# Two transformer blocks on one core: fp32 attention products as split fp32r products, and low parts of weights by adding transfers

## The chip, the cores and the metric

The kernel runs on one core of a Trainium2 chip. Its engines are TensorE (PE: matrix products and transposes, with the load of its stationary operand shown apart as PEld), VectorE (DVE), ScalarE (ACT), GpSimd (POOL) and SyncE (SP). Each executes its own instructions in a fixed order and waits on semaphores for the others. The metric is the device time of one execution in microseconds; before the change it is 1470.13 us, the median of three runs from 1469.56 to 1470.28.

## The reference

512 tokens of width 1024 pass two transformer blocks in fp32. Block 1 has two mixers, gated linear attention and a sparse attention (NSA: attention to compressed keys, to all earlier keys and to a window, with a softmax in each), and a gated feed-forward of width 2816. Block 2 has two short causal convolutions and a stick-breaking attention side by side, and a feed-forward of width 4096.

```python
# block 1
proj = rms_norm(x) @ w_in              # all projections of both mixers
x = x + rms_norm(mixed @ w_out)        # mixed: both mixers' outputs, gated
x = x + rms_norm((silu(h @ w_gate) * (h @ w_up)) @ w_down)
# block 2
p = _rmsnorm(x, g_attn) @ w_in         # a_b, a_c, a_h, b_glu, q, k, v
y_a = a_b * _causal_dwconv(a_c * a_h, w_conv_a)                    # 3 taps
y_b = silu(_layernorm(_causal_dwconv(glu(b_glu), w_conv_b) + b))   # 31 taps
x = x + concat([y_a, y_b, y_c]) @ w_out
x = x + square(relu(_rmsnorm(x, g_ffn) @ w_ff1)) @ w_ff2
```

y_c is the stick-breaking attention, eight heads of 64:

```python
def _stick_breaking(q, k, v):
    t_len = q.shape[2]
    scale = 1.0 / math.sqrt(q.shape[-1])
    outs = []
    for q0 in range(0, t_len, SB_BLOCK):
        kv_len = q0 + SB_BLOCK
        qb = q[:, :, q0:kv_len]
        kb = k[:, :, :kv_len]
        vb = v[:, :, :kv_len]
        z = jnp.einsum("bhqd,bhkd->bhqk", qb, kb).astype(jnp.float32) * scale
        t_idx = q0 + jnp.arange(SB_BLOCK)[:, None]
        s_idx = jnp.arange(kv_len)[None, :]
        mask = s_idx < t_idx
        log_beta = jax.nn.log_sigmoid(z)
        log_1m = jnp.where(mask, log_beta - z, 0.0)
        suffix = lax.cumsum(log_1m, axis=3, reverse=True) - log_1m
        a = jnp.where(mask, jnp.exp(log_beta + suffix), 0.0)
        outs.append(jnp.einsum("bhqk,bhkd->bhqd", a.astype(v.dtype), vb))
    return jnp.concatenate(outs, axis=2)
```

## The kernel before

A weight arrives in fp32 as a tile of 512 KB on SP's queue (`load`, L121, four buffers `wst`). `split_w` (L108) makes two tiles of type fp32r of it: the high part `whi` by a cast on ACT (L113) and the low part `wlo`, weight minus high part, on DVE (L114), four buffers each. Activations are split the same way (`split_psum`, L134 to L141, from PSUM: cast at L137, subtract at L138). A product of two fp32 matrices is then three fp32r products into one PSUM bank: high by high, low activation by high weight, high activation by low weight. `k_steps` (L160 to L162) does this for an output of 128 features by 512 tokens, eight weight blocks deep; `nat_steps` (L197 to L199) for one of 128 tokens by 512 features. Both are generators that give control back after each three products.

Some products of the attentions are not split but have fp32 operands. In block 1, `nsa_values` multiplies the values by the transposed weights of four key blocks; for the last block (b = 3, 128 columns) it uses an fp32 copy `VF` of the values and an fp32 `PTf` (L825), 16 times in all, while the other blocks use split parts. In block 2, `sb_scores` computes for every head and every query block j the scores z of 128 queries by 128 (j + 1) keys from fp32 `QF` and `KF` (L1076), and adds the causal mask by a bf16 product with an identity (L1077). ACT and DVE then turn z into weights: three functions on ACT (L1081 to L1083), a subtraction and a scan on DVE (L1085, L1086), an exp on ACT (L1089). `sb_values` transposes the weights on PE (L1114), splits them and multiplies them with the values, for the last key block from fp32 `VB3` (L1103). A trace shows an fp32 product as two records. In NSA's scores (L792) the width is a maximum of n and 256, so that none has fewer columns than that.

The order of the work in block 2's mixers is written as generators. `first_tiles` runs the first four weight tiles while the last norm of block 1 still transposes into hT (L384). Then a loop over the eight heads takes turns: a step of the head's values, some steps of `fill`, a convolution tap on DVE, a step of the next head's scores. `fill` is the sequence of everything else that PE has to do there: `v_steps` (v's columns in four chunks of 512 KB, used four times over), then pairs 1 to 3 of q and k, the convolutions' inputs (`glu_steps`, `gate_steps`), and the first part of the output projection. From the program in this order the framework's scheduler derives each engine's list, in which instructions may move against the written order; the lists are fixed before the run.

The norms go through ACT (squares, L349), POOL (`rstd`, L356 and L357) and DVE (`xn`, L378), then through PE's transposes.

Of the kernel before, what the change touches and what calls it, by code (L numbers as in the profile page):

```python
# [7 lines left out]
F32 = mybir.dt.float32  # L8
# [12 lines left out]
def kernel(  # L21
# [404 lines left out]
    VF = to("VF", shape=(128, 4, 64))  # L426
# [21 lines left out]
    def products(t):  # L448
        acc = ps("mm" if t < 3 else "s")
        nat_mm(hT_k, acc[:, 0:NM], t, wm)  # L450
        src = acc[:, 0:256].rearrange("p (b g d) -> p b g d", b=2, g=2)
        V.tensor_copy(misc[:, t, :], acc[:, 256:NM])
        split_psum(VS[:, t, :, :, 0, :], VS[:, t, :, :, 1, :], src)
        if t == 3:
            A.copy(VF.rearrange("p a d -> p (a d)"), acc[:, 0:256])

# [354 lines left out]
    def nsa_values(h, bi):  # L811

        g = h // 4
        tt = weights.pop((h, bi))
        parts = []

        def products():
            b, rhs = parts.pop(0)
            if b == 3:
# [12 lines left out]
        for b in (3, 2, 1, 0):  # L832
            n = 512 - 128 * b
            pt = ps("pt", "pt")
            for j in range(b, 4):
                nc.tensor.transpose(pt[:, (j - b) * 128:(j - b + 1) * 128],
                                    tt[j][:, b * 128:(b + 1) * 128], ident)
            if b < 3:
                ph = tS("PTh", F32R, bufs=2)
                pl = tS("PTl", F32R, bufs=2)  # L840
                split_psum(ph[:, 0:n], pl[:, 0:n], pt[:, 0:n])
                parts.append((b, (ph, pl)))
            else:
                pf = tS("PTf", shape=(128, 128), bufs=2)
                A.copy(pf, pt[:, 0:n])
                parts.append((b, (pf,)))
# [98 lines left out]
    def fin_mix(t, half, acc):  # L945
# [16 lines left out]
    identb = tc3("identb", BF16, (128, 128))  # L962
    V.tensor_copy(identb, ident)
    smask = tc3("smask", BF16, (128, 128))
    P.memset(smask, 0.0)
    P.affine_select(out=smask, in_=smask, compare_op=OP.is_gt, fill=-SBIG, base=0,
                    pattern=[[-1, 128]], channel_multiplier=1)
    cwa = tc3("cwa", shape=(128, 2, 3))
    cwb = tc3("cwb", shape=(128, 2, 31))

    def conv_weights():
        for src, dst, k in ((w_conv_a_2, cwa, 3), (w_conv_b_2, cwb, 31)):
            cn = t2("cn", shape=(k, 256))
# [70 lines left out]
    def pair_qk(i, accs):  # L1044
        QF[i], KF[i] = t3("QF", bufs=2), t3("KF", bufs=2)
        A.activation(QF[i], accs[0], AF.Copy, scale=0.125)
        A.copy(KF[i], accs[1])

    def pair_steps(i):
        accs = []  # L1050
        yield from tile_steps(accs, 1280 + i * 128)
        QF[i] = t3("QF", bufs=2)
        A.activation(QF[i], accs[0], AF.Copy, scale=0.125)
        yield from tile_steps(accs, 1792 + i * 128)
        KF[i] = t3("KF", bufs=2)
        A.copy(KF[i], accs[1])

    def v_steps():
        chunks = [([k, k + 1], load(w_in_2, k, 2, 2304, 512)) for k in range(0, 8, 2)]
        for t in range(4):  # L1060
            acc = ps()
            yield from nat_steps(hT_k, acc, t, chunks)
            src = acc.rearrange("p (h d) -> p h d", h=8)
            split_psum(VB[t][:, :, 0, :], VB[t][:, :, 1, :], src)
            if t == 3:
                A.copy(VB3, src)

    def sb_scores(h):

        i, u = h // 2, h % 2  # L1070
        r = slice(u * 64, u * 64 + 64)
# [21 lines left out]
    def sb_values(h):  # L1093
# [7 lines left out]
        def products(b, ph, pl):  # L1101
            if b == 3:
                mm(o[0:64, 384:512], VB3[:, h, :], ph, start=False, stop=False)  # L1103
                return
# [5 lines left out]
        for b in range(4):  # L1110
# [4 lines left out]
            if b < 3:  # L1115
                ph = t3("PTh", F32R, bufs=2)
                pl = t3("PTl0", F32R) if b == 0 else t3("PTl", F32R, bufs=2)
                split_psum(ph[:, 0:n], pl[:, 0:n], pt[:, 0:n])
                parts.append((b, ph, pl))
                pl0 = pl if b == 0 else pl0  # L1120
            else:
                pf = t3("PTf", shape=(128, 128))
                A.copy(pf, pt[:, 0:n])
                parts.append((b, pf, None))
# [8 lines left out]
        pv_evac(o, sby[0][r], t3("pvt", shape=(64, 512)))  # L1133
# [22 lines left out]
    def sigmoid(src):  # L1156
        th = t3("gth")
# [51 lines left out]
    def gate_steps(a):  # L1209
# [5 lines left out]
        m = t3("gam", shape=(128, 544))  # L1215
# [24 lines left out]
    pair_qk(0, accs[:2])  # L1240
    table("natural_log_exp_and_others")
    glu(0, accs[2:])

# [4 lines left out]
    fill = sequence(v_steps(), pair_steps(1), glu_steps(1), pair_steps(2), pair_steps(3), gate_steps(0),  # L1248
# [7 lines left out]
    for h in range(8):  # L1256
        scores = sb_scores(h + 1) if h < 7 else iter(())
        values = sb_values(h)
        for j in range(4):
            steps(values)  # L1260
            steps(fill, 2)
# [7 lines left out]
            steps(fill, 2)  # L1269
# [9 lines left out]
    def fp32_tile(t, h):  # L1279
        tag, bufs = (("QF", 2), ("KF", 2), ("sbe", 3), ("sbL", 2))[2 * h + t // 2]  # L1280
# [107 lines left out]
```

## Time and profile before

| | us |
|---|---|
| median of three runs | 1470.13 (1469.56 to 1470.28) |
| the profiled execution's own time | 1469.14 |
| its span, first to last instruction | 1467.4 |
| PE busy | 1448.1 (99%) |
| PEld busy | 1233.0 (84%) |
| DVE busy | 977.2 (67%) |
| ACT busy | 731.4 (50%) |
| POOL busy | 64.5 (4%) |
| mean granted clock of TensorE | 0.998 |

The span is the time from the first to the last instruction; busy time counts the time in which an engine executes at least one. PE's durations overlap, since products are pipelined: what one takes from PE is read from its start to the start of the next. Block 1's NSA attention lies between 255 and 410 us; block 2's first tiles end at about 912, its v products at 939, the heads at 1080.

### The profile page before, as it was taken

How to read it: one execution, taken by the hardware profiler on the slowest of the kernel's cores; microseconds unless marked ns; L12 is line 12 of the kernel's file. 1: busy time of each engine (PE TensorE's matmuls, PEld its weight loads, DVE VectorE, ACT ScalarE, POOL GpSimd, SP SyncE). 2: the span in 40 equal slices, each digit the busy share in tenths (PEclk: the TensorE clock that was granted, in tenths of full speed). 3: DMA queues.
4: the chain of work that ended last, by engine and by line, in shares of the span. 5: the costliest groups of instructions: out<-in, count | busy, mean ns of one | idle time of the engine just before them, and what ended most of it. 6: DMA issues, size and time to landing. Idle time of an engine off the chain costs nothing. (4 is left out here: it accounts for less than half of the span.)

```text
span 1467.4 us, 21573 instructions
## 1 busy us (share of the span) xinstructions
PE 1448.1 (99%) x8484; PEld 1233.0 (84%) x8484; DVE 977.2 (67%) x1607; ACT 731.4 (50%) x1294; POOL 64.5 (4%) x176
## 2 busy tenths in 40 slices
PE   8999999999999999999999999999999999999998
PEld 6788888787788889899889978766679989898996
DVE  5446556877755479579569845979767748384663
ACT  6434334666633266455335535577746527163453
POOL 2000002000000020000000021000101000000001
PEclk9999999999999999999999999999999999999999
DMA  8242222211133322324233522221122324233331
GB/s 235 74 115 58 73 73 72 58 44 58 44 115 115 113 74 88 119 83 115 87 114 97 179 71 79 80 59 58 58 86 58 115 75 131 83 92 109 88 130 58
DMA packets 181294, 133.30 MB, mean 91 GB/s; under 512 B 11765, under 2 KB 157239, under 8 KB 181192
## 3 DMA queue, kind: packets, MB, share of 16 engines
q1 hardware_dynamic: 181192, 131.92, 30.5%
q8 instruction: 67, 1.10, 0.3%
q14 instruction: 35, 0.29, 0.1%
HBM read 129.80 MB, written 2.10 MB: 90 GB/s over the span
## 5 line engine op out<-in xcount | busy, mean ns | idle before, releaser
L113 ACT CAST whi<-wst 128x1024 fp32r<-128x1024 f32 (+1 forms) x229 | 238.8, 1046 | 293.7 <-PE nat L187 140.1
L114 DVE TENSOR_TENSOR wlo<-wst,whi 128x1024 fp32r<-128x1024 f32 (+1 forms) x229 | 278.6, 1220 | 107.0 <-ACT whi L113 105.7
L263 PE MATMUL ps<-T,whi 128*128 128x256 f32 x1088 | 198.1, 283 | 0.9 <-ACT prod L299 0.9
L185 PE MATMUL nat<-whi,ah 128*128 128x512 f32 (+1 forms) x440 | 171.7, 390 | 0.0
L186 PE MATMUL nat<-wlo,ah 128*128 128x512 f32 (+1 forms) x440 | 171.2, 389 | 0.0
L187 PE MATMUL nat<-whi,al 128*128 128x512 f32 (+1 forms) x440 | 170.5, 390 | 0.0
L263 PEld LDWEIGHTS ps<-T,whi 128*128 128x128 f32 x1088 | 167.0, 188 | 1.4 <-ACT prod L299 1.3
L263 PE MATMUL ps<-T,wlo 128*128 128x256 f32 x544 | 153.2, 282 | 0.9 <-DVE wlo L114 0.9
L149 PE MATMUL ps<-hTh,whi 128*128 128x512 f32 (+1 forms) x336 | 115.9, 345 | 0.0
L150 PE MATMUL ps<-hTl,whi 128*128 128x512 f32 (+1 forms) x336 | 114.9, 342 | 0.0
L151 PE MATMUL ps<-hTh,wlo 128*128 128x512 f32 (+1 forms) x336 | 114.5, 341 | 0.0
L263 PEld LDWEIGHTS ps<-T,wlo 128*128 128x128 f32 x544 | 102.6, 189 | 1.0 <-DVE wlo L114 1.0
L187 PEld LDWEIGHTS nat<-whi,al 128*128 128x128 f32 x440 | 82.8, 188 | 18.7 <-DVE al L339 0.8
L185 PEld LDWEIGHTS nat<-whi,ah 128*128 128x128 f32 x440 | 82.8, 188 | 18.7 <-ACT ah L338 1.0
L160 PE MATMUL ps<-hTh,whi 128*128 128x512 f32 x240 | 98.0, 408 | 0.0
L186 PEld LDWEIGHTS nat<-wlo,ah 128*128 128x128 f32 x440 | 82.8, 188 | 17.7
L161 PE MATMUL ps<-hTl,whi 128*128 128x512 f32 x240 | 96.1, 400 | 0.0
L162 PE MATMUL ps<-hTh,wlo 128*128 128x512 f32 x240 | 95.8, 399 | 0.0
L1226 DVE TENSOR_TENSOR xt<-xt,nat 128x512 f32<-128x512 f32 x43 | 29.5, 685 | 79.0 <-PE nat L187 77.7
L263 PE MATMUL ps<-hTh,whi 128*128 128x256 f32 x272 | 76.9, 283 | 0.3 <-ACT whi L113 0.3
L263 PE MATMUL ps<-hTh,wlo 128*128 128x256 f32 x272 | 76.5, 281 | 0.0
L263 PE MATMUL ps<-hTl,whi 128*128 128x256 f32 x272 | 76.5, 281 | 0.0
(410 smaller groups left out, 3240.0 us busy)
## 6 DMA issues: line engine op xcount, KB each, us to landing
wst<-in_w_in_dram SPq DMA_DIRECT2D x70, 512.0 KB, 3.7
wst<-in_w_ff_dram SPq DMA_DIRECT2D x64, 512.0 KB, 4.3
wst<-in_w_ffn_gate_dram SPq DMA_DIRECT2D x22, 512.0 KB, 4.1
wst<-in_w_ffn_up_dram SPq DMA_DIRECT2D x22, 512.0 KB, 4.9
wst<-in_w_ffn_down_dram SPq DMA_DIRECT2D x22, 512.0 KB, 4.3
wst<-in_w_out_dram SPq DMA_DIRECT2D x16, 512.0 KB, 3.6
xt<-in_x_dram SPq DMA_DIRECT2D x8, 512.0 KB, 3.6
wst<-in_w_proj_gla_dram SPq DMA_DIRECT2D x8, 512.0 KB, 4.2
```

Source lines behind the costliest of these rows:

```text
L113: A.copy(hi, st)
L114: lo_eng[0].tensor_tensor(out=lo, in0=st, in1=hi.bitcast(F32), op=OP.subtract)
L149: mm(acc[:, ts], wh[:, k, cols], xh[:, k, ts], start=k == 0, stop=False)
L150: mm(acc[:, ts], wh[:, k, cols], xl[:, k, ts], start=False, stop=False)
L151: mm(acc[:, ts], wl[:, k, cols], xh[:, k, ts], start=False, stop=k == nk - 1)
L160: mm(acc, w[0][:, k], hT[0][:, k], start=k == 0, stop=False)
L161: mm(acc, w[0][:, k], hT[1][:, k], start=False, stop=False)
L162: mm(acc, w[1][:, k], hT[0][:, k], start=False, stop=k == 7)
L185: mm(acc, ah[:, s], wh[:, j, cols], start=i == 0, stop=False)
L186: mm(acc, ah[:, s], wl[:, j, cols], start=False, stop=False)
L187: mm(acc, al[:, s], wh[:, j, cols], start=False, stop=i == len(seq) - 1)
L263: mm(acc, w[a][:, k0 + k], x[b][:, k], start=first and k + i == 0, stop=last and k == 3 and i == 2, skip_group_check=True)
```

## The change

The fp32 products go. QF and KF become split parts: K is split for both heads of a pair at once (`Kh`, `Kl`), and Q into four zero-padded tiles of 128 rows, high and low for either head (`QZ`, named Qh and Ql in the lists). z is three fp32r products over 128 rows, and mask and identity are fp32r. The last key block's products use split values and split weights as the other blocks do, in both attentions. In a pair, k's tile now comes ahead of q's.

A part of the weights gets its low part in another way: ACT makes the high part (L135 of the changed kernel) and its negative (L136, into `wlo`), and a transfer on POOL's queue (L140) adds the weight from HBM to it. This holds for every second of the 22 tiles that follow the first four in block 2's mixers: two of v's four chunks, then one in two up to the output projection's first half. `wst` is still loaded, for the cast. In `fill`, gate 0 comes ahead of pair 3, and the steps per turn differ for some heads.

```diff
+    adding = [iter(())]
...
+        if next(adding[0], False):
+
+            hi, lo = (base.tile([128, kt, n], F32R, name=nm, tag=nm, bufs=4) for nm in ("whi", "wlo"))
+            A.copy(hi, st)
+            A.activation(lo, hi.bitcast(F32), AF.Copy, scale=-1.0)
+            for i in range(kt if step > 1 else 1):
+                k, j = (k0 + i * step, slice(i, i + 1)) if step > 1 else (k0, slice(0, kt))
+                src = w[k * 128:(k + j.stop - j.start) * 128, c0:c0 + n].rearrange("(k p) c -> p k c", p=128)
+                P.dma_start(out=lo[:, j], in_=src, accum_op=OP.add)
+            return hi, lo
...
-    VF = to("VF", shape=(128, 4, 64))
...
-                if bi == 0:
-                    o[0] = ps("o", "o")
-                    lhs = VCB[g][:, h % 4].rearrange("p a d -> p (a d)")
-                    mm(o[0], lhs, PCT[g][0], start=True, stop=False)
-                    mm(o[0], lhs, PCT[g][1], start=False, stop=False)
-                mm(o[0][0:64, b * 128:512], VF[:, 2 * bi + g, :], rhs[0], start=False, stop=False)
-                return
...
+            ph = tS("PTh", F32R, bufs=2)
+            pl = tS("PTl", F32R, bufs=2)
+            split_psum(ph[:, 0:n], pl[:, 0:n], pt[:, 0:n])
+            parts.append((b, (ph, pl)))
...
-    identb = tc3("identb", BF16, (128, 128))
-    V.tensor_copy(identb, ident)
-    smask = tc3("smask", BF16, (128, 128))
-    P.memset(smask, 0.0)
-    P.affine_select(out=smask, in_=smask, compare_op=OP.is_gt, fill=-SBIG, base=0,
+    identr = tc3("identr", F32R, (128, 128))
+    V.tensor_copy(identr, ident)
+    smask = tc3("smask", F32R, (128, 128))
+    mask = t2("cn", shape=(128, 256))[:, 0:128]
+    P.memset(mask, 0.0)
+    P.affine_select(out=mask, in_=mask, compare_op=OP.is_gt, fill=-SBIG, base=0,
                     pattern=[[-1, 128]], channel_multiplier=1)
+    V.tensor_copy(smask, mask)
...
-    QF, KF = {}, {}
+    KF = {}
-    VB3 = t3("VB3", shape=(128, 8, 64))
...
+    QZ = [[t3(f"Q{n}{u}", F32R) for n in "hl"] for u in range(2)]
+    none = t3("sbe", bufs=3)
+    P.memset(none, 0.0)
+    for u in range(2):
+        for q in QZ[u]:
+            A.copy(q[64 - 64 * u:128 - 64 * u], none[64 - 64 * u:128 - 64 * u])
...
+    def split_k(i, acc):
+        KF[i] = t3("Kh", F32R, bufs=2), t3("Kl", F32R, bufs=2)
+        split_psum(*KF[i], acc)
+
+    def split_q(acc):
+        for u in range(2):
+            r = slice(u * 64, u * 64 + 64)
+            split_psum(QZ[u][0][r], QZ[u][1][r], acc[r], scale=0.125)
...
+        yield from tile_steps(accs, 1792 + i * 128)
+        split_k(i, accs[0])
         yield from tile_steps(accs, 1280 + i * 128)
-        QF[i] = t3("QF", bufs=2)
-        A.activation(QF[i], accs[0], AF.Copy, scale=0.125)
-        yield from tile_steps(accs, 1792 + i * 128)
-        KF[i] = t3("KF", bufs=2)
-        A.copy(KF[i], accs[1])
+        split_q(accs[1])
...
-            mm(z[:, 0:n], QF[i][r, j * 128:(j + 1) * 128], KF[i][r, 0:n], start=True, stop=False)
-            mm(z[:, n - 128:n], identb, smask, start=False, stop=True)
+            for a, b in ((0, 0), (0, 1), (1, 0)):
+                mm(z[:, 0:n], QZ[u][a][:, j * 128:(j + 1) * 128], KF[i][b][:, 0:n], start=a + b == 0, stop=False)
+            mm(z[:, n - 128:n], identr, smask, start=False, stop=True)
...
-                mm(o[0:64, 384:512], VB3[:, h, :], ph, start=False, stop=False)
-                return
...
+    split_q(accs[0])
+    split_k(0, accs[1])
...
+    adding[0] = (i % 2 == 0 for i in range(22))
...
-    fill = sequence(v_steps(), pair_steps(1), glu_steps(1), pair_steps(2), pair_steps(3), gate_steps(0),
+    fill = sequence(v_steps(), pair_steps(1), glu_steps(1), pair_steps(2), gate_steps(0), pair_steps(3),
...
+        n1, n2 = (3, 3) if h == 3 else (2, 1) if h > 5 else (2, 2)
```

In the lists that follow, a row is an instruction with its line, kind, output <- inputs, and size. The first place is on PE, the start of pair 1's first weight tile behind v's products. Before (the transposes of head 0's weights stand just ahead; L160 to L162 are the tile's products, z head 1's first scores):

```order
L160 MATMUL ps<-hTh,whi 128x512
L161 MATMUL ps<-hTl,whi 128x512
L162 MATMUL ps<-hTh,wlo 128x512
L1076 MATMUL z<-KF,QF 128x128
L1077 LDWEIGHTS identb
L1077 MATMUL z<-smask,identb 128x128
L160 MATMUL ps<-hTh,whi 128x512
```

Now (L172 to L174 are the tile's products, L1085 z, L1086 the mask, L1120 transposes, L1112 the first product of head 0's values):

```order
L172 MATMUL ps<-hTh,whi 128x512
L173 MATMUL ps<-hTl,whi 128x512
L1085 MATMUL z<-Kh,Qh_8761 128x128
L1085 MATMUL z<-Kl,Qh_8761 128x128
L1085 MATMUL z<-Kh,Ql_8762 128x128
L1086 MATMUL z<-smask,identr 128x128
L1120 MATMUL pt<-ident,sbP_9102 128x128
L1120 MATMUL pt<-ident,sbP_9147 128x128
L1120 MATMUL pt<-ident,sbP_9192 128x128
L1085 MATMUL z<-Kh,Qh_8761 128x256
L1085 MATMUL z<-Kl,Qh_8761 128x256
L1085 MATMUL z<-Kh,Ql_8762 128x256
```

The first product with `wlo` has moved behind two blocks of scores, three transposes and a value product; it follows behind the second mask product and that value product, three rows after the last one shown. The second place is on POOL, the end of the norms of block 1 (rstd and sq) and the first memsets of block 2's heads. Before:

```order
L351 TENSOR_SCALAR sq<-sq 128x1
L356 TENSOR_TENSOR rstd<-sq 128x1
L357 TENSOR_TENSOR rstd<-rstd,nhalf 128x1
L356 TENSOR_TENSOR rstd<-sq 128x1
L357 TENSOR_TENSOR rstd<-rstd,nhalf 128x1
L1170 MEMSET G_8714 128x32
L1088 MEMSET sbP_8970 128x1
L1088 MEMSET sbP_9035 128x1
```

Now:

```order
L363 TENSOR_SCALAR sq<-sq 128x1
L368 TENSOR_TENSOR rstd<-sq 128x1
L369 TENSOR_TENSOR rstd<-rstd,nhalf 128x1
L140 DMA wlo<-in_w_in_dram 128x2x512
L368 TENSOR_TENSOR rstd<-sq 128x1
L369 TENSOR_TENSOR rstd<-rstd,nhalf 128x1
L1044 MEMSET sbe 128x512
L363 TENSOR_SCALAR sq<-sq 128x1
L1171 MEMSET G_8771 128x32
```

A transfer stands between two norms' rstd, and a memset of zeros that feeds the padding of Q stands behind the last of them shown. The third place is on ACT, where v's third chunk is cast, behind the load of a function table (gth belongs to the convolution's gate). Before:

```order
L400 ACT_TABLE_LOAD
L113 CAST whi<-wst 128x1024
L1151 ACTIVATE gth<-ps 128x512
L1152 ACTIVATE gth<-gth 128x512
L1153 ACTIVATE gth<-gth 128x512
L113 CAST whi<-wst 128x1024
```

Now:

```order
L412 ACT_TABLE_LOAD
L135 CAST whi<-wst 128x1024
L1152 ACTIVATE gth<-ps 128x512
L136 ACTIVATE wlo<-whi 128x1024
L1153 ACTIVATE gth<-gth 128x512
L113 CAST whi<-wst 128x1024
```

The negative of v's third chunk has come in behind the first gth row; the cast of the fourth chunk, which is not among the adding ones, follows it.

## Rows read from the trace of the kernel before

**Rows 1.** The page, part 1: PE's busy time, share of the span, instructions.
```profile
PE 1448.1 (99%) x8484; PEld 1233.0 (84%) x8484; DVE 977.2 (67%) x1607; ACT 731.4 (50%) x1294; POOL 64.5 (4%) x176
```

**Rows 2.** Busy time by stretch: its length, PE, PEld, DVE, ACT, POOL, clock, DMA share.
```profile
255.00:410.00 155.00, 154.37 (x806) 122.90 (x806) 115.33 (x390) 100.48 (x247) 0.00 (x0) 1.00 0.18 52
940.00:1040.00 100.00, 99.48 (x447) 67.61 (x446) 87.25 (x138) 68.12 (x141) 5.54 (x28) 1.00 0.24 71
```

**Rows 3.** PE's timeline (start, duration, line, shapes): filler products.
```profile
916.42 0.39 PE L198 MATMUL ps<-wlo,hTh 128*128 128x512 f32 x1
...
939.86 0.39 PE L161 MATMUL ps<-hTl,whi 128*128 128x512 f32 x1
940.09 0.40 PE L162 MATMUL ps<-hTh,wlo 128*128 128x512 f32 x1
...
975.27 0.39 PE L162 MATMUL ps<-hTh,wlo 128*128 128x512 f32 x1
```

**Rows 4.** PE's timeline around z of 512 columns.
```profile
988.35 0.39 PE L162 MATMUL ps<-hTh,wlo 128*128 128x512 f32 x1
988.66 1.12 PE L1076 MATMUL z<-KF,QF 64*128 64x512 f32 x2
...
990.08 0.39 PE L160 MATMUL ps<-hTh,whi 128*128 128x512 f32 x1
```

**Rows 5.** PE's timeline around z of 128 columns.
```profile
994.20 0.40 PE L161 MATMUL ps<-hTl,whi 128*128 128x512 f32 x1
994.53 0.48 PE L1076 MATMUL z<-KF,QF 64*128 64x128 f32 x2
...
995.30 0.39 PE L160 MATMUL ps<-hTh,whi 128*128 128x512 f32 x1
```

**Rows 6.** PE's timeline around L825, block 1.
```profile
276.98 0.38 PE L836 MATMUL pt<-ident,P 128*128 128x128 f32 x2
277.29 0.43 PE L825 MATMUL o<-PTf,VF 128*64 128x128 f32 x2
277.66 0.44 PE L836 MATMUL pt<-ident,P 128*128 128x128 f32 x2
```

**Rows 7.** PE's timeline around L1103, block 2.
```profile
991.23 0.39 PE L162 MATMUL ps<-hTh,wlo 128*128 128x512 f32 x1
991.55 0.43 PE L1103 MATMUL o<-PTf,VB 128*64 128x128 f32 x2
...
992.25 0.38 PE L1114 MATMUL pt<-ident,sbP 128*128 128x128 f32 x2
```

**Rows 8.** The page, parts 3 and 6: q1's packets, MB, share; w_in's loads.
```profile
q1 hardware_dynamic: 181192, 131.92, 30.5%
...
wst<-in_w_in_dram SPq DMA_DIRECT2D x70, 512.0 KB, 3.7
```

**Rows 9.** ACT's timeline: casts of four weight tiles, one gth.
```profile
910.00 1.05 ACT L113 CAST whi<-wst 128x1024 fp32r<-128x1024 f32 x1 [0.83 <-PE ps L150]
...
911.58 0.63 ACT L1152 ACTIVATE gth<-gth 128x512 f32<-128x512 f32 x1
...
935.26 2.07 ACT L113 CAST whi<-wst 128x1024 fp32r<-128x1024 f32 x2
...
947.21 1.05 ACT L113 CAST whi<-wst 128x1024 fp32r<-128x1024 f32 x1 [0.17 <-PE ps L161]
```

**Rows 10.** DVE's timeline: the first subtract of v's tiles, idle before it.
```profile
911.08 1.23 DVE L114 TENSOR_TENSOR wlo<-wst,whi 128x1024 fp32r<-128x1024 f32 x1 [10.88 <-ACT whi L113]
```

**Rows 11.** POOL's timeline in the norm that ends block 1.
```profile
894.98 1.43 POOL L357 TENSOR_TENSOR rstd<-rstd,nhalf 128x1 f32<-128x1 f32 x1
```

**Rows 12.** DVE by line in the heads: busy us, mean ns, idle before.
```profile
L780 DVE TENSOR_TENSOR sby<-o,pvt 64x512 f32<-64x512 f32 x5 | 3.4, 675 | 0.5 <-ACT pvt L779 0.5
```

**Rows 13.** PE's timeline around a 64-column fp32r product.
```profile
246.37 0.19 PE L751 MATMUL sc<-KC,QSp 128*128 128x64 f32 x1
246.40 0.47 PE L719 MATMUL ps<-hTh,whi 128*128 128x512 f32 x1
```

More of the change, by code (lines that the diff above doesn't have):

```diff
@@ L453, in products @@
         split_psum(VS[:, t, :, :, 0, :], VS[:, t, :, :, 1, :], src)
-        if t == 3:
-            A.copy(VF.rearrange("p a d -> p (a d)"), acc[:, 0:256])
     norm_T(0, g_pre, hT)
@@ L818, in products @@
             b, rhs = parts.pop(0)
-            if b == 3:
-                if bi == 0:
-                    o[0] = ps("o", "o")
-                    lhs = VCB[g][:, h % 4].rearrange("p a d -> p (a d)")
-                    mm(o[0], lhs, PCT[g][0], start=True, stop=False)
-                    mm(o[0], lhs, PCT[g][1], start=False, stop=False)
-                mm(o[0][0:64, b * 128:512], VF[:, 2 * bi + g, :], rhs[0], start=False, stop=False)
-                return
+            if b == 3 and bi == 0:
+                o[0] = ps("o", "o")
+                lhs = VCB[g][:, h % 4].rearrange("p a d -> p (a d)")
+                mm(o[0], lhs, PCT[g][0], start=True, stop=False)
+                mm(o[0], lhs, PCT[g][1], start=False, stop=False)
             lhs = VS[:, b, bi, g].rearrange("p a d -> p (a d)")
@@ L837, in nsa_values @@
                                     tt[j][:, b * 128:(b + 1) * 128], ident)
[L838 to L846, printed above, removed]
+            ph = tS("PTh", F32R, bufs=2)
+            pl = tS("PTl", F32R, bufs=2)
+            split_psum(ph[:, 0:n], pl[:, 0:n], pt[:, 0:n])
+            parts.append((b, (ph, pl)))
             yield
@@ L972, in conv_weights @@
         for src, dst, k in ((w_conv_a_2, cwa, 3), (w_conv_b_2, cwb, 31)):
-            cn = t2("cn", shape=(k, 256))
+            cn = t2("cn", shape=(128, 256))[0:k]
             nc.sync.dma_start(cn, src[0])
@@ L1064, in v_steps @@
             split_psum(VB[t][:, :, 0, :], VB[t][:, :, 1, :], src)
-            if t == 3:
-                A.copy(VB3, src)
     def sb_scores(h):
         i, u = h // 2, h % 2
-        r = slice(u * 64, u * 64 + 64)
         sticks[h] = []
@@ L1101, in products @@
         def products(b, ph, pl):
-            if b == 3:
-                mm(o[0:64, 384:512], VB3[:, h, :], ph, start=False, stop=False)
-                return
             lhs = VB[b][:, h].rearrange("p a d -> p (a d)")
@@ L1114, in sb_values @@
                 nc.tensor.transpose(pt[:, (j - b) * 128:(j - b + 1) * 128], pts[j][:, b * 128:(b + 1) * 128], ident)
[L1115 to L1124, printed above, removed]
+            ph = t3("PTh", F32R, bufs=2)
+            pl = t3("PTl0", F32R) if b == 0 else t3("PTl", F32R, bufs=2)
+            split_psum(ph[:, 0:n], pl[:, 0:n], pt[:, 0:n])
+            parts.append((b, ph, pl))
+            pl0 = pl if b == 0 else pl0
             yield
@@ L1132, in sb_values @@
             sby[0] = t3("sby")
-        pv_evac(o, sby[0][r], t3("pvt", shape=(64, 512)))
+        pv_evac(o, sby[0][r], t3("pvt", shape=(64, 512), tag="PTl0"))
         if u:
@@ L1156, in sigmoid @@
     def sigmoid(src):
-        th = t3("gth")
+        th = t3("gth", shape=(128, 544))[:, 0:512]
         log_sigmoid(th, src, th)
@@ L1214, in gate_steps @@
         c = t3("gac")
-        m = t3("gam", shape=(128, 544))
+        m = t3("gam", shape=(128, 544), tag="gth")
         P.memset(m[:, 0:32], 0.0)
@@ L1239 @@
     accs = first_tiles([(w_in_2, 1280, "mm"), (w_in_2, 1792, "mm"), (w_in_2, 1024, "mm"), (w_in_2, 768, "s")], ahead)
-    pair_qk(0, accs[:2])
+    split_q(accs[0])
+    split_k(0, accs[1])
     table("natural_log_exp_and_others")
     glu(0, accs[2:])
+    adding[0] = (i % 2 == 0 for i in range(22))
     def sequence(*gens):
@@ L1258 @@
         values = sb_values(h)
+        n1, n2 = (3, 3) if h == 3 else (2, 1) if h > 5 else (2, 2)
         for j in range(4):
             steps(values)
-            steps(fill, 2)
+            steps(fill, n1)
             conv_taps(1)
@@ L1268 @@
             steps(values)
-            steps(fill, 2)
+            steps(fill, n2)
             conv_taps(1)
@@ L1279, in fp32_tile @@
     def fp32_tile(t, h):
-        tag, bufs = (("QF", 2), ("KF", 2), ("sbe", 3), ("sbL", 2))[2 * h + t // 2]
+        tag, bufs = (("Kh", 2), ("Kl", 2), ("sbe", 3), ("sbL", 2))[2 * h + t // 2]
         FQ[h, t] = t3("F", shape=(128, 4, 128), tag=tag, bufs=bufs)
```

4 lines of the change are left out of this document (removed).

## The prediction

> **What bounds the kernel now.** I read the page's totals first. PE is busy in 1448.1 of 1467.4 us [rows 1], so the end is set by the sum of what PE executes plus a few waits. Then the busy time by stretch: in block 1's attention (255 to 410 us) DVE is busy 115.33 and ACT 100.48 of 155 us, so there is room beside PE; in block 2's heads (940 to 1040 us) DVE has 87.25 of 100 us and ACT 68.12 [rows 2]. A product less is therefore a gain on the path almost one to one, as long as two things hold: that the new splitting keeps up on DVE, and that no product comes to wait for an operand. Last I read PE's timeline around the fp32 products, start to start, since PE's starts give what an instruction takes from the path better than its modelled duration.
>
> **What the removed fp32 products cost.** A 512-column product with fp32r operands takes 0.23 us from start to start [rows 3]. The product before starts at 988.35 [rows 4] and should end its share at 988.58; z starts at 988.66, and after z, its mask product and two 256-column products (0.12 each, half of 0.23) the next filler starts at 990.08. So z and mask with their changes of mode take 990.08 - 988.35 - 0.23 - 0.24 = 1.26 us at 512 columns. At 128 columns, 994.20 to 995.30 less two fillers is 0.64 us [rows 5]. The 256- and 384-column ones lie on the line between: 0.85 and 1.06. A head has one of each: 3.81 us, and eight heads 30.5 us.
>
> New: z as three fp32r products and an fp32r mask product of 128 columns. At the filler's rate three of 512, 384 and 256 columns take 0.69, 0.52 and 0.35. For 128 columns I take 0.11: two 128-column transposes and the change to fp32 (0.08, as above) fill 276.98 to 277.29 [rows 6]. So 3 x 0.11 = 0.33, four masks 0.44, together 2.33 a head and 18.6 in all. Saved: 30.5 - 18.6 = **11.9 us**.
>
> The last key block's product (L1103 in block 2) takes 992.25 - 991.23 less two 512-column ones (0.46) = 0.56 us [rows 7]; its two fp32r products take 0.22, so 0.34 x 8 = **2.7 us**. L825 in block 1 takes 277.66 - 276.98 - 0.22 = 0.46 [rows 6], new 0.22: 0.24 x 16 = **3.8 us**. PE loses 18.4 us together. The bounds of this term: an fp32r product of 128 columns costs at least its columns' share, 0.06, which would save 5 us more over all that are new, and at most what an fp32 one streams; that I price as a rival.
>
> **The added transfers.** Eleven weight tiles get no subtract on DVE; ACT makes the high part and its negative, and a transfer on POOL's queue adds the weight. The trace has no transfer on POOL's queue at all: nearly all bytes go through q1 [rows 8], so its time X, from the end of the negative to the low part's arrival, has to be bounded. The nearest row is a plain 512 KB load on SP's queue, 3.7 us [rows 8]. It is the lower end, since the accumulating one moves the same bytes and reads the sum besides; above, three times that (it reads the weight, reads the sum and writes it) is 11 us. I take X = 6, nearer to the low row since one load keeps little of the DMA engines busy in this stretch.
>
> The Trainium skill ("Collectives: The Full Stack", Why ReduceScatter is half of AllGather) says an add in the transfer needs two source reads and measured a ratio of 1.93 to a copy; an estimate by that page is 7 us, and the sum would come out 2 us later. No row here shows an accumulating transfer.
>
> Where does X matter? Most tiles are ready long ahead: ACT casts one at 947.21, and the product with its low part comes at 975.27 [rows 3, 9], 28 us later. Two are tight. The second transferred tile is v's third chunk, cast at 910.00 and used by L198 at 916.42 [rows 3, 9]. In ACT's new order one gth instruction stands between the cast and the negative, so the negative begins where the gth at 911.58 stood and ends at 912.6; the transfer leaves at 912.7. PE comes 0.2 earlier to its first use, by the one z block of 128 columns before it, so it waits X - 3.5 = 2.5 us. The other is the first tile of pair 1. ACT casts two tiles from 935.26 to 937.33 and comes to the negative behind both, 1.05 later: it ends at 938.4. On PE the order puts z (0.44), three transposes (0.33), z again (0.47) and a value product (0.23) between L161's successor, at 939.86 before [rows 3], and the first low product: 939.86 + 0.23 + 1.47 = 941.6, less some 0.4, since the transpose ahead of it awaits an exp whose scan no longer stands behind a subtract on DVE: 941.2. PE waits X - 2.8 = 3.2 us. Together **5.7 us**, 2X - 6.3: at X = 3.7 it is 1.1, at 11 it is 15.7. Behind the waiting transfer POOL has memsets of single columns for later heads, which ACT needs some 10 us later.
>
> The first transfer sits on POOL between two rstd pairs of the norm that ends block 1. Issuing it may hold POOL, and ACT has one negative (1.05) and four zero copies of 64 partitions (0.6 each) more to do in that norm, whose rstd and squares PE's transposes wait for through xn. I take 0.5 us; bounds 0 to 3.
>
> POOL and DVE may disturb each other: an rstd of 128x1 elements took 1.43 us at 894.98 [rows 11]. The Trainium skill ("SBUF — State Buffer", 🔬 SBUF: two separate sides) says that GpSimd cannot write the descriptors of a transfer from its own queue while DVE runs an operation in its two-port mode, and advises ACT's or SP's queue. By this rule X is longest where DVE is densest, in the heads; that is the slow transfer among the rivals, and no row here tells how long.
>
> **DVE and ACT in the heads.** From DVE go, behind the two early tiles, 9 of the 11 subtracts at 1.22 [rows 10]: -11.0 us. To it come, for three pairs, the split of K (0.68) and two of Q (0.68 each, as the 64-partition L780 does [rows 12]), 6.1 us, and eight 128-column splits (about 0.25), 2.0. So DVE's work falls by 3 while PE's falls by 14: its share rises from 87% to some 94 to 97% of the heads. ACT gains 11 negatives of 1.05 and three casts of 64 partitions: about 13 us, to 85%. Waits follow in two ways. First crowding: a fill tile's cast or a stick's scan comes late now and then; bounds 0 to 5, taken 1.5. Second the new Q: its acc is finished, ACT casts (0.6), DVE subtracts (0.68), and only then z can start; before it was one ACT copy of K. In PE's new order 2.2, 2.9 and 2.4 us of other products lie between Q's last product and z for pairs 1 to 3, against 0.2 + 0.6 + 0.7 + some 0.3 of handing over = 1.8 without any queue; an instruction in progress on DVE (mean about 0.7) eats the cover of pair 1. I take 0.7 for each, **2 us**, bounds 0 to 6. In block 1 DVE gets 16 splits of about 0.25 in 155 us with 40 free, hidden beside PE; the copies that fed the fp32 products go from ACT as casts of the same size come. The new order of the fill (gate 0 ahead of pair 3) and of its steps keeps their number in the heads, 128, so PE finds as much to do between the sticks: nothing.
>
> **Sum.** Own time of the profiled execution 1469.14 - 18.4 (products) + 5.7 (two tight tiles) + 0.5 (POOL) + 3.5 (crowding and Q) = 1460.4. The median of the runs is 1.0 above that execution: **1461 us**, 0.6% less than 1470.13. The lowest end: X = 3.7, no crowding, 1469.14 - 18.4 + 1.1 + 1.0 = 1453.
>
> **Rivals.**
> *The transfer is slow.* If POOL cannot write its descriptors beside DVE, or the sum's read and write run one behind the other, X grows, and both tight tiles pay it twice over: no change at 2X - 6.3 = 14.4, X = 10.4; from X = 11.8 it is slower by over 0.2%, and at X = 15 the time is 1479. Above some 25 the other nine come late too. For it: that rstd [rows 11], and DVE busy nearly all the time in the heads; against: DVE came from 10.88 us of idleness when it began its subtract at 911.08 [rows 10], and in the v products around the first tight tile it is far from dense. Chance 0.10.
> *Narrow fp32r products stream at the fp32 rate.* NSA's scores are computed to at least 256 columns (the width is a maximum of n and 256), which hints at such a cost. One of the two passes of a 128-column fp32 product takes 0.21 (0.43 for both [rows 7]); then 3 + 4 products a head and 2 x 24 last-block ones each cost 0.10 more: 5.6 + 4.8 = 10.4 us, 1471.5. Against it: a 64-column fp32r product is followed 0.03 us later by the next [rows 13], its columns' share at the full rate. Chance 0.06.
> *DVE becomes the bound of the heads.* With 97% of a shortened stretch, every wait of a DVE instruction for ACT comes through to PE. If DVE reaches no more than 91% (it reached 87% with PE in front), 87 us of work need 96 us and not 90: 5 to 6 us more than the sum, less the 1.5 for crowding, 1465 to 1467. Chance 0.22.
>
> **How the numbers follow.** The forecast's own case, 1454 to 1465, has 0.62. A comparison of this kernel tells 0.2%, 2.9 us, from no change. Faster than 1467.2: the forecast, 0.18 of the DVE rival, none of the others: 0.80. Same, 1467.2 to 1473: 0.04 of the DVE rival, the narrow products' 0.06, and 0.02 of a transfer about X = 10: 0.12. Slower: the other 0.08 of the slow transfer. The range reaches from 1452 to 1470, which leaves out X above 10 or so and some of the narrow case.
>
> **What would show it.** Right: L1085's three products a block with starts 0.23 apart at 512 columns and 0.11 at 128; PE waiting for a DMA at its first L210 of the third chunk and its first L174 of pair 1, 2 to 4 us each, and at no later tile; waits of z for Ql under 1 us. Wrong: a median transfer on POOL's queue over 10 us, or L174 waiting in later tiles; 128-column products 0.2 apart; more than 5 us of PE waits for DVE between 940 and 1070.

## The result, and where the time went

The changed kernel takes 1478.21 us (median of four runs, 1475.21 to 1478.68) against 1470.20, a ratio of 1.0051 with a 95% interval of 1.0034 to 1.0068. The forecast was 1461 with a range of 1452 to 1470 and gave "slower" 8 in 100. The profiled execution took 1477.9 us, 8.8 more than the one before. On its page PE's busy time is 9.3 us below that of [rows 1], about half of the 18.4 that the forecast took off for the products, and a second queue stands beside q1 [rows 8], with the accumulating loads in the rows on DMA issues (the last column is the median from issue to landing).

```profile
PE 1438.8 (97%) x8516; PEld 1249.5 (85%) x8516; DVE 978.1 (66%) x1633; ACT 742.9 (50%) x1311; POOL 79.2 (5%) x188
...
q0 software_dynamic: 8368, 5.77, 2.9%
...
wlo<-in_w_in_dram POOLq DMA_DIRECT2D x9, 512.0 KB, 6.3
```

So 9.3 us of PE's busy time went and 18 us of other time came. I therefore cut the span at the same events. First the stretches of the changed kernel (columns as in [rows 2]): the start, NSA's attention, and block 2's mixers from the first z to the last product of a head's values, here called the heads.

```profile
10.00:50.00 40.00, 37.69 (x180) 29.79 (x181) 25.68 (x45) 26.27 (x48) 3.26 (x7) 0.87 0.60 170
258.70:407.40 148.70, 148.28 (x792) 122.63 (x793) 116.26 (x399) 97.54 (x242) 0.00 (x0) 1.00 0.18 54
912.40:1088.30 175.90, 157.82 (x769) 127.77 (x768) 140.78 (x229) 119.50 (x235) 20.23 (x44) 0.97 0.43 92
```

The same stretches of the kernel before:

```profile
10.00:50.00 40.00, 37.24 (x190) 29.43 (x191) 26.38 (x47) 27.21 (x51) 3.35 (x7) 0.96 0.61 170
256.40:408.20 151.80, 151.74 (x793) 120.88 (x794) 113.25 (x383) 98.28 (x243) 0.00 (x0) 1.00 0.18 53
912.90:1079.90 167.00, 166.00 (x736) 114.97 (x735) 143.18 (x221) 110.75 (x223) 6.58 (x33) 1.00 0.22 67
```

NSA is 3.1 us shorter. The heads are 8.9 us longer although PE has less to do there: it idles 18.1 us where it idled 1.0, and its mean granted clock is 0.97. The start is 2.3 us longer (NSA begins at 258.7 in place of 256.4), by a clock of 0.87 for 0.96 over nearly the same work. That is no part of the change, for it differs among kernels whose start is the same: of the profiled runs below, e1, e4 and e8 begin NSA at 256.3 to 256.6 us, e2 and e9 at 257.6 to 257.9, the others at 258.5 to 259.5. Without it the two profiled runs differ by 6.5 us. (The mean clock was 0.995 to 0.999 over the runs of before, 0.992 in three of the four here and 0.996 in the one of 1475.21 us.) What PE waited for between 912.4 and 1088.3 (total, times, longest):

```profile
PE ps L174 <- DMA wlo<-in_w_in_dram: 6.7, 1, 6.7
PE pt L1120 <- ACT sbP L1098: 6.4, 6, 1.4
PE ps L210 <- DMA wlo<-in_w_in_dram: 2.2, 1, 2.2
PE z L1085 <- DVE sbe L1095: 1.1, 2, 0.7
```

Three things, then. **Transfers**: 2.2 us at v's third chunk and 6.7 at pair 1's first tile, the two that the forecast named, and at no later tile. From issue to landing the first took 5.8, the second 9.4, and one issued at 960.2, with one plain load still under way, 6.3 (the view of wlo on POOL, a window around each):

```profile
DMA to landing us min/median/max: 5.8/5.8/5.8
...
DMA to landing us min/median/max: 9.4/9.4/9.4
...
DMA to landing us min/median/max: 6.3/6.3/6.3
```

**Clock**: behind each of the two waits PE ran at 1.2 GHz for some 3 us of products; in the second the granted clock had fallen while PE still waited (0.62 over 946 to 950). By stretch, and then on PE's timeline, where products follow every 0.23 us after the wait and from 919.86 on every 0.43:

```profile
917.00:919.00 2.00, 0.71 (x3) 0.61 (x4) 1.92 (x3) 0.00 (x0) 0.00 (x0) 1.00 1.08 285
919.00:921.00 2.00, 2.00 (x8) 1.57 (x7) 0.75 (x1) 0.00 (x0) 0.00 (x0) 0.67 0.09 28
921.00:923.00 2.00, 2.00 (x8) 1.71 (x8) 0.15 (x1) 0.60 (x2) 0.00 (x0) 0.50 0.00 0
946.00:950.00 4.00, 0.00 (x0) 0.00 (x0) 4.00 (x8) 1.52 (x4) 0.00 (x0) 0.62 1.30 226
952.00:954.00 2.00, 2.00 (x7) 1.57 (x6) 0.00 (x0) 0.00 (x0) 0.00 (x0) 0.54 1.23 278
```

```profile
918.29 0.50 PE L210 MATMUL ps<-wlo,hTh 128*128 128x512 f32 x1 [2.24 <-DMA wlo<-in_w_in_dram]
918.63 0.40 PE L211 MATMUL ps<-whi,hTl 128*128 128x512 f32 x1
918.87 0.39 PE L209 MATMUL ps<-whi,hTh 128*128 128x512 f32 x1
...
919.86 0.63 PE L210 MATMUL ps<-wlo,hTh 128*128 128x512 f32 x1
920.29 0.63 PE L211 MATMUL ps<-whi,hTl 128*128 128x512 f32 x1
```

**Sticks**: six waits of about 1.1 us, one in most heads, for the last exp of a head's weights. The products alone (first experiment) show it best, so the rows of that chain stand there.

### The profile page after: what moved, and what is told of

Its sections match the earlier page's. It is cut to its first block, busy times and chain, and to the rows that moved or that the text cites. A ratio compares the mean times of both kernels' runs of the same rounds, so it can differ in the third digit from the quotient of the medians.

```text
span 1476.2 us, 21708 instructions
## 1 busy us (share of the span) xinstructions
PE 1438.8 (97%) x8516; PEld 1249.5 (85%) x8516; DVE 978.1 (66%) x1633; ACT 742.9 (50%) x1311; POOL 79.2 (5%) x188
## 5 line engine op out<-in xcount | busy, mean ns | idle before, releaser
L113 ACT CAST whi<-wst 128x1024 fp32r<-128x1024 f32 (+1 forms) x218 | 227.4, 1046 | 291.7 <-PE nat L199 140.5
L114 DVE TENSOR_TENSOR wlo<-wst,whi 128x1024 fp32r<-128x1024 f32 (+1 forms) x218 | 265.2, 1220 | 99.3 <-ACT whi L113 98.5
L162 PE MATMUL ps<-hTl,whi 128*128 128x512 f32 (+1 forms) x336 | 114.9, 342 | 0.0
L174 PE MATMUL ps<-hTh,wlo 128*128 128x512 f32 x240 | 96.7, 403 | 6.7 <-DMA wlo<-in_w_in_dram 6.7
L172 PE MATMUL ps<-hTh,whi 128*128 128x512 f32 x240 | 98.4, 410 | 0.0
```

What stands on the lines that cost most here:

```text
L113: A.copy(hi, st)
L114: lo_eng[0].tensor_tensor(out=lo, in0=st, in1=hi.bitcast(F32), op=OP.subtract)
L162: mm(acc[:, ts], wh[:, k, cols], xl[:, k, ts], start=False, stop=False)
L172: mm(acc, w[0][:, k], hT[0][:, k], start=k == 0, stop=False)
L174: mm(acc, w[1][:, k], hT[0][:, k], start=False, stop=k == 7)
```

## Experiments

All medians with the ratio to the kernel before on the same chip, and the heads of each profiled run (length, PE busy, mean clock):

| kernel | us | ratio, 95% | heads: length, PE busy, clock |
|---|---|---|---|
| before | 1470.2 | | 167.0, 166.0, 1.00 |
| changed | 1478.21 | 1.0051 (1.0034 to 1.0068) | 175.9, 157.8, 0.97 |
| e1 products only | 1469.04 | 0.9994 (0.9986 to 1.0003) | 167.3, 156.0, 0.99 |
| e2 transfers only | 1482.11 | 1.0082 (1.0069 to 1.0096) | 179.6, 170.7, 0.97 |
| e3 no tight tiles | 1468.95 | 0.9984 (0.9974 to 0.9993) | 166.3, 156.2, 0.99 |
| e4 filled waits | 1477.45 | 1.0045 (1.0031 to 1.0059) | 173.6, 164.0, 1.00 |
| e5 products, cover | 1468.79 | 0.9990 (0.9982 to 0.9999) | 168.0, 155.9, 1.00 |
| e6 few taps | 1465.64 | one run | 163.6, 154.2, 1.00 |
| e7 late transfers, cover | 1467.51 | 0.9982 (0.9972 to 0.9993) | 167.3, 157.3, 0.99 |
| e8 the same, more cover | 1469.20 | 0.9995 (0.9986 to 1.0004) | 169.4, 159.9, 0.99 |
| e9 short chain | 1465.47 | 0.9964 (0.9951 to 0.9977) | 165.2, 155.6, 0.99 |
| e10 products, more fill | 1471.81 | 1.0004 (0.9995 to 1.0013) | 174.3, 163.5, 0.98 |
| e11 late transfers, more fill | 1468.11 | 0.9985 (0.9977 to 0.9994) | 170.1, 160.2, 1.00 |
| e12 short chain, few taps | 1461.86 | 0.9937 (0.9920 to 0.9955) | 160.4, 154.2, 1.00 |

**e1, the products alone** (with the new order of `fill` and its new steps per turn, which stay).

```diff
-    adding[0] = (i % 2 == 0 for i in range(22))
+    adding[0] = iter(())
```

> All of the change but the adding transfers: every low part comes from DVE's subtract again. Theory A (the loss is two PE waits for transfers, 2.2 and 6.7 us, and half a clock for some 3.5 us behind each; the products save what the prediction said): those 8.9 us and about 3 us of slow clock go, the six waits for sticks of 6.4 us stay, so 1464 to 1468 us, and no stretch of half clock between 905 and 1090. Rival B (DVE's added splits are the bound of the heads, and eleven subtracts more make it worse): 1472 us or more, waits of PE for ACT's sbP and for DVE well over 10 us. Rival C (the narrow fp32r products save nothing): 1470 or more with PE busy near 1448.

No change: the gain in the heads is lost without any transfer. That is 1 us above theory A's range, and the clock did fall once in these heads (from 955.6 on), which theory A had ruled out; rivals B (1472 or more) and C (PE busy near 1448; it is 1435.0) fare worse. NSA keeps its gain, and in the heads PE works 10 us less and idles 10 us more: 7.1 us of it for sbP, in seven waits.

```profile
PE pt L1120 <- ACT sbP L1098: 7.1, 7, 1.4
PE z L1085 <- DVE sbe L1095: 1.1, 2, 0.7
PE z L1085 <- DVE Ql L153: 0.8, 1, 0.8
```

DVE's busy time between 975 and 1035, before and then here:

```profile
975.00:1035.00 60.00, 60.00 (x269) 40.69 (x269) 56.35 (x91) 40.39 (x85) 2.35 (x15) 1.00 0.17 53
975.00:1035.00 60.00, 56.30 (x284) 46.35 (x282) 58.94 (x93) 40.80 (x83) 2.58 (x14) 1.00 0.20 62
```

Its rows from one z of 512 columns to the transpose of its weights:

```profile
985.69 0.22 PE L1086 MATMUL z<-smask,identr 128*128 128x128 f32 x1
985.95 0.59 ACT L1090 ACTIVATE sbe<-z 128x512 f32<-128x512 f32 x1
...
988.32 0.68 DVE L1094 SCALAR_TENSOR_TENSOR sbL<-z,sbe 128x512 f32<-128x512 f32 x1
988.92 0.67 DVE L153 SCALAR_TENSOR_TENSOR Ql<-ps,Qh 64x512 fp32r<-64x512 f32 x1
...
989.52 1.20 DVE L1095 TENSOR_TENSOR_SCAN sbe<-z,sbL 128x511 f32<-128x511 f32 x1
...
990.84 0.63 ACT L1098 ACTIVATE sbP<-sbe 128x511 f32<-128x511 f32 x1 [0.32 <-DVE sbe L1095]
...
991.52 0.33 PE L1120 MATMUL pt<-ident,sbP 128*128 128x128 f32 x1 [1.01 <-ACT sbP L1098]
```

And of the kernel before, a head later:

```profile
1007.35 0.23 PE L1077 MATMUL z<-smask,identb 128*128 128x128 bf16 x1
...
1009.76 0.68 DVE L1085 SCALAR_TENSOR_TENSOR sbL<-z,sbe 128x512 f32<-128x512 f32 x1
...
1012.75 0.63 ACT L1089 ACTIVATE sbP<-sbe 128x511 f32<-128x511 f32 x1
...
1013.61 0.60 PE L1114 MATMUL pt<-ident,sbP 128*128 128x128 f32 x4
```

The chain is as long in both, 5.8 us (985.69 to 991.47) and 6.0 (1007.35 to 1013.38). Before, PE's products reached to 1013.6 and just covered it. Now they end a microsecond early, for two reasons of about 0.7 us each. An fp32 z of 128 columns and the fp32 product of the last block lay in that interval, and what stands there now is shorter. And 18 filler products lay there, where now there are 15: the scheduler has put the transposes that wait for the exp further forward in PE's list. It did so in the neighbouring heads too: from the second head's weights to the sixth's, 18, 16, 22, 18 and 15 filler products before, 12, 12, 15, 15 and 12 here. The filler that follows in the list stays behind while PE waits at the transpose. The chain contains the new subtract Ql in the place of another instruction of the same length.

**e2, the transfers alone**, on the kernel before (the branch in `load` and the line that sets `adding`).

> The kernel before with the adding transfers alone (same eleven tiles, fp32 products kept). Theory A: two PE waits of 2 to 8 us for the transfer and a slow clock behind each, nothing gained, since PE is the bound: 1478 to 1484 us. Rival B (DVE is what the heads wait for, so that eleven subtracts less help): 1470 or less.

Slower by 0.8%, as theory A has it, by which the loss lies with the transfers: waits of 2.1 and 5.5 us, a clock of 0.97 in the heads, and eleven subtracts less on DVE win nothing.

**e3, without the two tight tiles.**

```diff
+    adding[0] = (i % 2 == 0 and i not in (2, 4) for i in range(22))
```

> The changed kernel, but v's third chunk and the first tile of pair 1 keep DVE's subtract; nine tiles are added by transfer. Theory A: both waits for transfers and the half clock behind them are gone, 12 us less than the changed kernel: 1464 to 1468. Rival B (sticks and DVE): 1472 or more, since the waits for sticks stay and DVE has two subtracts more. Rival D (any transfer on POOL's queue delays the heads, through shared DMA engines or POOL): 1472 or more with new waits for other tiles.

Both waits for transfers are gone, and nine transfers cost and bring nothing against e1. The new waits for other tiles that rival D expected did not come. The median lies 1 us above the range of theory A, which had counted the waits for sticks in (6.8 us here); the eleven runs spread from 1465.8 to 1470.3, and in the profiled one the clock fell once in the heads, about a wait for a stick.

**e4, the waits filled.** The lines added ahead of the waiting product (`zr` is a tile of zeros; idle is 30 for pair 1's first tile, 10 for the v chunk):

```diff
+            for _ in range(idle if k == 0 else 0):
+                mm(acc, zr[0], hT[0][:, k], start=False, stop=False)
```

> The changed kernel with products by a tile of zeros put in front of the two waiting products (10 for v's third chunk, 30 for pair 1's first tile, added into the same bank), so that PE is busy while the transfers run. The transfers land when they did. Theory A: no half clock follows, and the kernel gains the slow products' excess, about 3 us: 1474 to 1476. Rival E (the clock falls for another reason than the wait): half clock in the same places and 1478 or more.

```profile
942.00:950.00 8.00, 8.00 (x40) 6.57 (x39) 5.53 (x9) 1.63 (x6) 1.06 (x2) 1.00 1.29 234
950.00:960.00 10.00, 10.00 (x52) 8.43 (x51) 4.40 (x8) 6.98 (x14) 1.75 (x3) 1.00 0.57 119
```

No slow clock follows, and the heads are 2.3 us shorter than the changed kernel's with 9.2 us (40 x 0.23) more on PE: the clock fell because PE waited. The runs spread from 1473.5 to 1480.29 about a median of 1477.45, so the total does not show 3 us.

**e5, e7, e8, cover moved.** On e1 (e5) and e3 (e7, e8), filler goes behind the fourth block of scores:

```diff
-            steps(fill, n2)
+            steps(fill, n2 + ((-2, -2, -1, 5)[j] if h < 7 else 0))
```

(e8: -2, -2, -2, 6.)

> The products alone, with filler steps moved within each head: fewer behind the first three blocks of scores and five more behind the fourth (512 columns), so that some 5.9 to 6.5 us of PE work instead of 4.2 to 4.6 lie between that z and the transpose of its weights. Theory F (the stick's chain of about 6 us from z to its last exp was just covered by PE's work before, 5.5 to 7.2 us, and the shorter products took the cover away): the waits for sbP fall from 7.1 to 1 or 2 us, 1463 to 1465 us. Rival B (DVE's load is what PE waits for): the waits come back at other blocks, 1468 or more.

> The changed kernel without the two tight transfers, with the filler moved as in the run with products and cover. Theory F: the waits for sbP go here too, 1462 to 1465 us; beside the products with cover it tells whether nine transfers are worth anything at all: by F nothing, within 2 us. Rival B: faster by 3 us or more than the products with cover, since DVE has nine subtracts less.

> The same with six steps moved instead of five: 6.6 to 7.2 us of PE work between the z of 512 columns and its transpose, and fewer fillers between the other blocks. Theory F: no wait for sbP of the fourth block is left, 1461 to 1464; where the shorter distances of the other blocks become too short, waits of z for the scan (DVE's sbe) come in their place and it is no faster than the one with five.

Theory F, by which the products lack cover at one place of the head, missed in all three: 6.3 us of waits for sbP stayed in e5. Filler lies there again (in the head shown 23 products), but the chain has grown: when z of 512 columns is done, ACT still has a weight tile's cast and a split's cast ahead in its list. Its first function starts 1.5 us after z, and the last exp ends at 991.0, 7.8 us after z.

```profile
983.22 0.23 PE L1086 MATMUL z<-smask,identr 128*128 128x128 f32 x1
983.28 1.04 ACT L113 CAST whi<-wst 128x1024 fp32r<-128x1024 f32 x1
...
984.21 0.58 ACT L149 CAST Kh<-ps 128x512 fp32r<-128x512 f32 x1
...
984.69 0.61 ACT L1090 ACTIVATE sbe<-z 128x512 f32<-128x512 f32 x1
...
990.37 0.63 ACT L1098 ACTIVATE sbP<-sbe 128x511 f32<-128x511 f32 x1 [0.92 <-DVE sbe L1095]
```

So filler in this one interval is not enough, since the same lists also set when the chain can run. That a loop through a whole head is too long for PE's work would fit, but is not shown. e7 is 1.3 us below e5, within the 2 us that theory F allowed nine transfers, and not the 3 of rival B.

**e6, e9, e12, what the loop consists of**, all on e1. e6 keeps 11 of 31 taps per half of the convolution; e9 has one exp with a scale of zero for the three functions between z and sbL; e12 has both.

```diff
-    taps = [(a, k) for a in range(2) for k in range(31)]
+    taps = [(a, k) for a in range(2) for k in range(11)]
```

```diff
-            A.activation(e[:, 0:n], z[:, 0:n], AF.Abs)
-            A.activation(e[:, 0:n], e[:, 0:n], AF.Exp, scale=-1.0)
-            A.activation(e[:, 0:n], e[:, 0:n], AF.Ln, bias=1.0)
+            A.activation(e[:, 0:n], z[:, 0:n], AF.Exp, scale=0.0)
```

> The products alone, and 40 of the 62 convolution taps left out (their part of the convolution is missing from the output), which takes some 28 us from DVE in the heads. Theory F: the chain from z to exp keeps at least 5.3 us and the waits for sbP stay at 4 us or more. Rival B (DVE's load): DVE under 80% busy, and the waits for sbP fall below 2 us.

> The products alone, with one function on ACT in place of the three between z and the subtraction (so the weights of the sticks are not the reference's): the chain from z of 512 columns to its last exp loses 1.3 us, and ACT some 14 us in all. PE's and DVE's work stays. Theory F (each head waits for that chain, which PE's work no longer covers): 1.0 to 1.3 us less in each of seven heads, 1459 to 1462 us, and the time from z to the transpose of its weights falls by as much, even where the scheduler puts less PE work between. Rival B (throughput of DVE, or PE's own work, decides): 1467 or more.

> The products alone, with both cuts of the runs before together: one function on ACT in place of three in the stick's chain, and 40 of the 62 convolution taps left out. Each alone took some 2 us from the heads. Theory G (two limits of nearly the same length lie right under PE's: the stick's chain of about 6 us per head, and DVE, which is 95 to 99% busy from 975 to 1035 us; either one alone holds the heads when the other goes): both together give clearly more than the sum of the two, the heads fall by 6 us or more from 165.6 (without slow clock) and PE's idle time in them from 11.3 to 5 or less, 1458 to 1462 us. Theory H (the waits come from something that neither cut touches, as the buffers of z or the layer norm): 4 us or less together, idle time of 8 or more, 1464 or more.

The heads, e6, e9 and e12, a fence each:

```profile
912.70:1076.30 163.60, 154.20 (x770) 125.58 (x768) 123.80 (x198) 112.30 (x225) 5.68 (x34) 1.00 0.22 68
```

```profile
911.30:1076.50 165.20, 155.59 (x769) 126.14 (x768) 148.82 (x238) 84.58 (x161) 5.59 (x34) 0.99 0.22 67
```

```profile
912.00:1072.40 160.40, 154.23 (x770) 125.13 (x768) 124.82 (x198) 84.67 (x162) 5.84 (x34) 1.00 0.23 70
```

In e6 the waits for sbP stayed at 5.7 us, as theory F had it (4 or more; rival B: under 2). e9 ended between its theories (1459 to 1462, or 1467 or more). 25 us off DVE take 2 us from the heads (163.6 against 165.6, e1's 167.3 less 1.7 for its slow clock), 27 us off ACT and a chain 1.3 us shorter take 2 as well, both together 5.2. Neither DVE's load nor the chain alone is the answer, so rival B and theory F are each half right. Theory G's 6 us and its idle time of 5 were just missed (5.2 and 6.2). The scheduler also moves the transposes forward when the chain is shorter, so its gain is partly given back: in the five heads counted above e9 has 10, 8, 13, 13 and 8 filler products there and e12 has 8, 8, 13, 11 and 8, and PE still waits 0.2 to 2.2 us at each. So the place of the transposes in PE's list is a third suspect beside the chain and DVE. No run holds that place fixed, and what holds the last 6 us is open.

**e10, e11, more filler in the last heads**, on e1 and e3.

```diff
+                    half_steps(yT, w_out_2, [2, 3], fin_add, 0))
...
-        n1, n2 = (3, 3) if h == 3 else (2, 1) if h > 5 else (2, 2)
+        n1, n2 = (3, 3) if h == 3 else (3, 2) if h == 5 else (2, 1) if h > 6 else (2, 2)
...
-    nat_half(yT, w_out_2, [2, 3, 6, 7], fin_add, 0)
+    nat_half(yT, w_out_2, [6, 7], fin_add, 0)
```

> The products alone, and eight steps of the output projection more (the two blocks of the long convolution, 5.5 us of PE work) moved from behind the heads into the last three. Theory F: filler where PE waits is free, so some 2 to 4 us of the waits in the last heads go, less for four more additions on DVE: 1465 to 1467 us. Rival B: the same work only moves, 1469.

> The same on the changed kernel without the two tight transfers. Theory F: 2 to 4 us below that kernel's 1469, 1465 to 1467, and equal to the products with more fill within 2 us. Rival B: 1469; or, if the nine subtracts that DVE is spared matter, 3 us or more below the products with more fill.

The work only moved: idle time in the heads is 10.8 and 9.9 us, and theory F missed both times. e11 lies 3.7 us below e10, which rival B would put down to the subtracts that DVE is spared; but the idle times differ by 0.9 only, and the clock in e10's heads is 0.98 for 1.00, so the slow clock accounts for most of it.

Of the versions with the whole computation e3, e7 and e11 beat both kernels, by 0.15 to 0.18%, and e5 by 0.10%. That is 1.5 to 2.7 us, no more than the 3 us that NSA gained.

## Why the prediction was wrong

- *The products* were right: NSA 3.5 us less PE work (forecast 3.8); the heads 11.7 less at full clock (166.0 against 157.8 less half of some 6.9 us at 1.2 GHz), forecast 14.6. A wait is counted from the modelled end of the product before and so hides about 0.17 us in busy time; some fifteen of them would make up most of the difference (an estimate). In a row of fp32r products one of 128 columns takes 0.11 us, as forecast: twice its share of the 0.23 us for 512 columns, but half of the 0.21 that the rival needed. That rival is dead. In the changed kernel:

```profile
967.32 0.28 PE L1085 MATMUL z<-Kl,Qh 128*128 128x128 f32 x1
967.43 0.27 PE L1085 MATMUL z<-Kh,Ql 128*128 128x128 f32 x1
967.54 0.28 PE L1086 MATMUL z<-smask,identr 128*128 128x128 f32 x1
```

- *The tight tiles* were the right two with nearly the right slack (5.8 - 2.2 = 3.6 and 9.4 - 6.7 = 2.7 us, forecast 3.5 and 2.8), and X = 6 was right for nine of the eleven transfers, 5.8 to 6.5. For pair 1's tile it was 9.4 and for the next one 10.5: they were issued within 4 us, with two plain loads between them. That makes 8.9 us in place of 5.7. What slowed them is not isolated: in e2 the same tile took 9.5 with two plain loads beside it and the next accumulating one only 6.3 us later, but the one issued at 888.8 here had three plain loads beside it and landed after 6.4. The Trainium skill ("Collectives: The Full Stack", Why ReduceScatter is half of AllGather) says that the add needs two source reads and has a measured ratio of 1.93; here the medians are 6.3 and 3.7 us, 1.7, but of two different queues. From the Trainium skill's "SBUF — State Buffer" (🔬 SBUF: two separate sides) I took the dense heads for the worst place. Dense work on DVE was not enough for that: the one issued at 994.6, into 7 us of which DVE was busy 6.82, landed after 6.2 us, and those at 1010.9, 1025.2 and 1073.4, beside work as dense, after 6.1 to 6.5. The rule is about operations in a two-port mode, and the trace does not tell an operation's mode.
- *The clock* had no term in the sum. Behind the two waits it cost 3.4 us, and the start, with a lower clock by chance, 2.3.
- *The failed step* is "a product less is therefore a gain on the path almost one to one", with the waits that "DVE and ACT in the heads" allowed beside it: crowding 1.5 and Q 2 us. Measured: 8.2 us more idle time in the changed kernel beside the transfers, 10.3 in e1, so that the removed products shortened e1's heads by 1.4 us only (167.0 to 165.6, at full clock). The waits were not those that the step had priced: for Ql 0.8 us at most (e1), for the last exp of a head's weights 6.4 (7.1 in e1). I read that PE waited for nothing in the heads of before, and took that for slack; but in the head shown the chain from z to the last exp had 0.2 us to spare (0.05 to 0.8 over the eight heads), and DVE was at 94% between 975 and 1035. I priced the cover of the new Q, and not the cover that the removed products had given. The same step put the new order of the fill at nothing, since the number of its steps in the heads stays 128; where the chain runs, 3 to 7 filler products fewer lie in PE's list of e1 (the five heads counted above). How much of the idle time is due to each is open.
- The rival *DVE becomes the bound* had the right size for the idle time (5 to 6 us above the sum; 8.2 and 10.3 are 4.7 and 6.8 above the 3.5 that the sum held) with half of the mechanism. Its time was added up wrongly: 1461 plus 5 to 6 less 1.5 is 1464.5 to 1465.5, not 1465 to 1467. The slow transfer, priced with X alone, needed X = 10.4 for no change; with the clock and the sticks beside it 9.4 on one tile was enough. Of the signs of being wrong that the forecast named none showed; PE's waits for DVE stayed at 2.7 us, and the ones that counted were for ACT's exp.

Sum of the profiled runs: -3.1 (NSA), +8.9 (heads: -11.7 products, +8.9 transfers, +8.2 other waits, +3.4 clock), +2.3 (start), +0.7 (elsewhere) = +8.8, as measured; the parts of the heads are rounded.

## What to carry to other kernels

An engine that is 99% busy is the bound only up to the next limit: before counting a removed instruction as gained, follow the longest chain that its neighbours cover, and take the spare time at the end of that chain as the first guess of what can be gained there. Here the spare times of the eight heads add up to 2.1 us, and e1's heads became 1.4 us shorter. Then look where the scheduler has put the waiting instruction in the new list, and not only how much work there is in all. A transfer that replaces a subtract belongs only on tiles whose lead exceeds its time beside other transfers, and a wait of PE has to be priced with the slow products behind it.

## What the runs showed of the hardware

An accumulating load of 512 KB by POOL's queue took 5.8 to 6.5 us from issue to landing in nine of eleven cases of the changed kernel, most with another load under way, and 9.4 and 10.5 for two that were issued 3.5 us apart; its issue holds POOL for 1.2 to 1.6 us. In the changed kernel's heads PE's granted clock fell to 1.2 GHz about a wait of 2.2 us and in one of 6.7, in e1 and e3 about two waits close together (0.8 and 1.4 us; 0.4 and 1.5), in e7 and e8 likewise (1.2 and 0.8), in e9 about one of 2.2, and at two places in e10. In e4's heads it did not fall: there zero products filled the two long waits. An fp32r product of 128 columns takes 0.11 us in a row of such, one of 256 columns 0.12, one of 512 columns 0.23.
